# Score products of a chunked linear recurrence on TensorE: eight batches a head become four

## The chip, the cores and the metric

The kernel runs on one core of one Trainium2 chip. The metric is the device time of one execution, in microseconds (us); the time before is the median of three runs.

## The reference, cut to what matters

Two layers act on 256 context tokens and 512 latent tokens of width 1024. Layer 0 is a bidirectional gated linear recurrence with 16 heads (key size 128, value size 128), layer 1 a gated linear scan; each has an RMS norm, an adaLN modulation from a condition vector, and a gated residual. The change lies in layer 0. Per head, token t reads token s of its chunk with a decay that is a product of forget gates between s and t, per key channel:

```python
b = jnp.cumsum(gc, axis=2)
diff = b[:, :, :, None, :] - b[:, :, None, :, :]
decay = jnp.exp(jnp.where(lower_tri, diff, -jnp.inf))
scores = jnp.einsum('bhtk,bhsk,bhtsk->bhts', qc, kc, decay)
o = (jnp.einsum('bhts,bhsv->bhtv', scores, vc)
     + jnp.einsum('bhtk,bhkv->bhtv', qc * jnp.exp(b), S))
```

The adaLN step is `sc @ ada_w[i] + ada_b[i]`, split in shift, scale and gate.

## The kernel before

Tokens lie along the free dimension (768 of them, six chunks of 128), channels along the 128 partitions. Weights come from memory in tiles of 128 x 1024 (`raw`); ScalarE rounds each to `hi`, VectorE takes the rest `lo`, and each projection is three matmuls (`mm3`, lines L311 to L313: hi by hi, hi by the rest, rest by hi).

`hgrn(h, side)` computes a head. The scores of a chunk are built without an exponential of a difference: level l (0 to 6, B = 2^l) gives the products between neighbouring blocks of B tokens. For that, `KK` (keys of both directions) and `QQ` (queries of both directions) are multiplied in place, level by level, by the gates of the blocks, whose products are the tiles `T`. One level is:

- TensorE: the products `lv` (L460), 24 small column-tiled matmuls of 32 keys by 32 queries (12 of 64 by 64 in level 6), with the gathered keys `kt` as weights and a view of `QQ` as the moving side; they go to four column groups of the array (`tile_position`). `dg` (L440) are the products of the diagonal, made the same way ahead of level 0.
- VectorE: the update of `KK` (L464), the next `T` (L469), the update of `QQ` (L471; it has to wait until the products of this level have read `QQ`), and for levels 0 to 4 a masked copy of the products into `D` (L474).
- ScalarE: the gather of the next level's keys from `KK` into `kt` (L415), and for levels 5 and 6 the copy of the products into the score tile `A` (L479); after level 4 it copies `D` into `A` (L483).

While head h is in `hgrn`, TensorE's main work is the filler: projections of head h + 1 (`in`, `v`) and output projections of earlier heads (`o`). `interleave` hands out filler in proportion to the weights that `hgrn` yields; the yields of the levels are the places where filler goes between batches. In some heads a `side` generator advances one adaLN step (`ada_block`: four column-tiled matmuls at L230, later four transposes `adat` at L240) at each level:

```python
next(side, None)
```

The engines run their queues in order. A planning layer sets each engine's order from the program order and its own estimate of readiness. PSUM tiles of `dg`, `lv`, `ada`, `kT`, `U` and `o` come from one pool of four (`atile`), those of the filler from another of four (`dtile`).

## Time and profile before

| | |
|---|---|
| median of 3 runs | 1603.09 us (1602.52 to 1603.98) |
| profiled execution, its time | 1605.08 us |
| its span, first to last instruction | 1603.3 us |
| TensorE busy | 1549.6 us, 97% of the span |
| VectorE busy | 1203.0 us, 75% |
| ScalarE busy | 856.5 us, 53% |
| mean granted TensorE clock | 0.985 of full |

Busy time counts an instruction from its start to its modelled end, so the starts of neighbouring matmuls tell more about TensorE than their durations do. In the timeline, "x48" means that many records in a row from one line and tile; a matmul of 32-bit floats appears as two records (two passes), so 24 products are 48.

### The profile page before, as it was taken

How to read it: one execution, taken by the hardware profiler on the slowest of the kernel's cores; microseconds unless marked ns; L12 is line 12 of the kernel's file. 1: busy time of each engine (PE TensorE's matmuls, PEld its weight loads, DVE VectorE, ACT ScalarE, POOL GpSimd, SP SyncE). 2: the span in 40 equal slices, each digit the busy share in tenths (PEclk: the TensorE clock that was granted, in tenths of full speed). 3: DMA queues.
4: the chain of work that ended last, by engine and by line, in shares of the span. 5: the costliest groups of instructions: out<-in, count | busy, mean ns of one | idle time of the engine just before them, and what ended most of it. 6: DMA issues, size and time to landing. Idle time of an engine off the chain costs nothing.

```text
span 1603.3 us, 33990 instructions
## 1 busy us (share of the span) xinstructions
PE 1549.6 (97%) x14740; PEld 1430.2 (89%) x14740; DVE 1203.0 (75%) x1867; ACT 856.5 (53%) x1359; POOL 11.8 (1%) x16
## 2 busy tenths in 40 slices
PE   5999999999999999999999999998999999999995
PEld 3899999999999999999999999987888888888884
DVE  4767678768867867767876776686768887797898
ACT  4554444444443453444444445544578578667874
POOL 0000000000000000000000000001000000000001
PEclk9999999999999999999999999997999999999997
DMA  8231211110211211223132231301122222322211
GB/s 323 84 115 53 94 54 40 54 54 28 77 44 41 67 40 54 61 86 106 39 109 58 76 120 29 105 28 53 53 67 79 67 79 66 93 64 68 80 53 53
DMA packets 33861, 116.79 MB, mean 73 GB/s; under 512 B 3633, under 2 KB 6065, under 8 KB 33713
## 3 DMA queue, kind: packets, MB, share of 16 engines
q1 hardware_dynamic: 32192, 113.26, 22.4%
q8 instruction: 116, 1.90, 0.5%
q10 hardware_dynamic: 1520, 1.37, 0.3%
q14 instruction: 33, 0.26, 0.1%
HBM read 112.52 MB, written 2.10 MB: 71 GB/s over the span
## 4 chain that ended last, share of the span: by engine, by line
PE 85%; DVE 9%; ACT 3%; issue 1%; DMA 0%; POOL 0%; POOLq 0%; DVEq 0%; ACTq 0%
PE in L311 12%; PE in L312 11%; PE in L313 11%; PE v L381 8%; PE lv L460 4%; PE o L536 4%; PE r L313 3%; PE r L311 3%; PE r L312 3%; PE o L311 3%; PE o L312 3%; PE o L313 3%; PE U L504 2%; PE gt L311 2%; PE gt L312 2%; PE gt L313 2%
## 5 line engine op out<-in xcount | busy, mean ns | idle before, releaser
L311 PE MATMUL in<-h_hi,hi 128*128 128x384 f32 x1024 | 354.8, 348 | 3.4 <-ACT h_hi L304 2.7
L312 PE MATMUL in<-h_lo,hi 128*128 128x384 f32 x1024 | 345.9, 338 | 0.4 <-DVE h_lo L305 0.3
L313 PE MATMUL in<-h_hi,lo 128*128 128x384 f32 x1024 | 345.0, 337 | 0.0
L129 ACT ACTIVATE hi<-raw 128x1024 fp32r<-128x1024 f32 x160 | 168.4, 1057 | 167.3 <-PE in L312 59.5
L130 DVE TENSOR_TENSOR lo<-raw,hi 128x1024 fp32r<-128x1024 f32 x160 | 194.9, 1219 | 77.1 <-ACT hi L129 76.9
L311 PEld LDWEIGHTS in<-h_hi,hi 128*128 128x128 f32 x1024 | 192.7, 188 | 20.2 <-issue 8.6
L312 PEld LDWEIGHTS in<-h_lo,hi 128*128 128x128 f32 x1024 | 193.1, 189 | 2.9 <-issue 1.6
L313 PEld LDWEIGHTS in<-h_hi,lo 128*128 128x128 f32 x1024 | 192.7, 188 | 0.9 <-issue 0.4
L471 DVE TENSOR_TENSOR QQ<-QQ,T 128x768 f32<-128x768 f32 x112 | 117.6, 1050 | 73.3 <-PE lv L460 73.3
L415 ACT ACTIVATE kt<-KK 128x768 f32<-128x768 f32 x112 | 102.2, 913 | 54.3 <-DVE KK L464 46.7
L313 PE MATMUL r<-h_hi,lo 128*128 128x512 f32 (+1 forms) x344 | 123.8, 360 | 3.7 <-DVE lo L130 3.7
L464 DVE TENSOR_TENSOR KK<-KK,T 128x768 f32<-128x768 f32 x112 | 117.1, 1045 | 9.6 <-ACT kt L415 9.5
L312 PE MATMUL r<-h_lo,hi 128*128 128x512 f32 (+1 forms) x344 | 123.2, 358 | 0.0
L337 ACT ACTIVATE sg<-in 128x384 f32<-128x384 f32 x128 | 61.7, 484 | 115.0 <-PE in L313 114.8
L311 PE MATMUL r<-h_hi,hi 128*128 128x512 f32 (+1 forms) x344 | 123.0, 358 | 0.0
L381 PE MATMUL v<-hi,h_hi 128*128 128x256 f32 x384 | 112.3, 292 | 0.0
L381 PE MATMUL v<-lo,h_hi 128*128 128x256 f32 x384 | 107.4, 280 | 0.0
L381 PE MATMUL v<-hi,h_lo 128*128 128x256 f32 x384 | 107.4, 280 | 0.0
L405 DVE SCALAR_TENSOR_TENSOR x<-o,ada,x 128x256 f32<-128x256 f32 (+1 forms) x184 | 82.1, 487 | 12.9 <-PE o L313 12.5
L559 DVE RECIPROCAL sq<-sq 128x384 f32<-128x384 f32 x30 | 75.9, 2540 | 21.0 <-ACT sq L553 21.0
L311 PE MATMUL o<-rhi,hi 128*128 128x384 f32 (+2 forms) x240 | 87.0, 364 | 2.2 <-DVE lo L130 1.2
L460 PEld LDWEIGHTS lv<-QQ,kt 128*32 128x32 f32 (+1 forms) x4992 | 63.4, 113 | 28.6 <-issue 20.8
(202 smaller groups left out, 3257.8 us busy)
## 6 DMA issues: line engine op xcount, KB each, us to landing
raw<-in_hgw_dram SPq DMA_DIRECT2D x64, 512.0 KB, 3.7
raw<-in_ada_dram SPq DMA_DIRECT2D x48, 512.0 KB, 4.3
raw<-in_rgi_dram SPq DMA_DIRECT2D x32, 512.0 KB, 4.1
raw<-in_hgv_dram SPq DMA_DIRECT2D x16, 512.0 KB, 3.9
raw<-in_hgo_dram SPq DMA_DIRECT2D x16, 512.0 KB, 3.8
raw<-in_rgg_dram SPq DMA_DIRECT2D x16, 512.0 KB, 3.6
raw<-in_rgo_dram SPq DMA_DIRECT2D x16, 512.0 KB, 3.9
x<-in_x_dram SPq DMA_DIRECT2D x8, 384.0 KB, 5.9
```

The costliest lines, as they stand in the source:

```text
L129: self.nc.scalar.activation(hi, r, AF.Copy)
L130: self.nc.vector.tensor_tensor(lo, r, hi.bitcast(F32), ALU.subtract)
L311: PE.matmul(ps, lhsT=wh, rhs=xh, start=first and i == 0, stop=False, skip_group_check=skip)
L312: PE.matmul(ps, lhsT=wh, rhs=xl, start=False, stop=False, skip_group_check=skip)
L313: PE.matmul(ps, lhsT=wl, rhs=xh, start=False, stop=last and i == n - 1, skip_group_check=skip)
L381: PE.matmul(ps, lhsT=xh[:, kk, t], rhs=w[:, k], start=part == 0 and k == 0 and i == 0 and c % 2 == 0, stop=part == 1 and k == 3 and i == 2 ...
L405: V.scalar_tensor_tensor(xs, ps[:, a - c.start:b - c.start], gate[:, d, 1 - j:2 - j], xs, ALU.mult, ALU.add)
L415: A.activation(view(kt, 0, [[2 * B, n], [B, 2], [1, B]]), view(KK, 0, [[2 * B, n], [NT + B, 2], [1, B]]), AF.Copy)
L460: PE.matmul(ps[w * g:w * g + w, w * c:w * c + w], lhsT=kt[:, o:o + w], rhs=rhs, start=c == 0, stop=c == NC - 1, skip_group_check=True, til ...
L464: V.tensor_tensor(kv, kv, view(T, 1, [[2, n], [m - 1, 2], [0, B]]), ALU.mult)
L471: V.tensor_tensor(qv, qv, view(T, m + 1, [[2, n], [-m - 1, 2], [0, B]]), ALU.mult)
L559: V.reciprocal(rs, rs)
```

## The change

Levels are taken two by two. At an odd level (1, 3, 5) nothing goes to TensorE; its queries are copied out of `QQ` into a tile of their own, `qt`, before `QQ` is updated, and its keys stay in their `kt`. At the following even level (2, 4, 6) the products of both levels are issued back to back. The diagonal products are issued just ahead of level 0, with no yield between. The adaLN step is called at even levels only, so four times a head, behind the joint batch; what is left of it runs at the end of the head. The scores are read from PSUM (masked copies, copies into `A`) after the even level's updates. A pool of two buffers is added for `qt`, and the scratch for dynamically issued DMA is made smaller.

```diff
-    qqp, kkp, gsp, ktp = p0("qqp", 2), p0("kkp", 2), p0("gsp", 2), p0("ktp", 3)
+    qqp, kkp, gsp, ktp, qtp = p0("qqp", 2), p0("kkp", 2), p0("gsp", 2), p0("ktp", 3), p0("qtp", 2)
...
-        A.activation(D, ps[:, :32 * NC].rearrange("p (c t) -> p c t", c=NC), AF.Copy)
-        yield 1.5
-        T = s["T0"]
-        for l in range(NLEV):
+        def products(l, kt, qt):
             B = 1 << l
-            n = NT // (2 * B)
-            m = NT // B
             ps = atile(f"lv{h}_{l}")
             w = 64 if B == 64 else 32
             for c in range(NC):
                 for g in range(P // w):
                     o = P * c + w * g
-                    if B < 32:
+                    if qt is not None:
+                        rhs = qt[:, o:o + w]
+                    elif B < 32:
                         rhs = view(QQ, o, [[2 * B, 16 // B], [NT + B, 2], [1, B]])
...
+        def scores(l, ps):
...
+        T = s["T0"]
+        waiting = None
+        for l in range(NLEV):
+            B = 1 << l
+            n = NT // (2 * B)
+            m = NT // B
+            first = l % 2 == 1
+            if first:
+                qt = qtp.tile([P, NT], F32, name=f"qt{h}_{l}", tag="qt")
+                if B == 32:
+                    A.activation(view(qt, 0, [[2 * B, n], [1, B]]), view(QQ, NT + B, [[2 * B, n], [1, B]]), AF.Copy)
+                    A.activation(view(qt, B, [[2 * B, n], [1, B]]), view(QQ, 0, [[2 * B, n], [1, B]]), AF.Copy)
+                else:
+                    gather(QQ, qt, B)
+                waiting = (l, kt, qt)
+            else:
+                pss = [(waiting[0], products(*waiting))] if waiting else []
+                pss.append((l, products(l, kt, None)))
+                next(side, None)
+                if l == 0:
+                    A.activation(D, dg[:, :32 * NC].rearrange("p (c t) -> p c t", c=NC), AF.Copy)
+            kv = view(KK, 0, [[2 * B, n], [NT + B, 2], [1, B]])
+            V.tensor_tensor(kv, kv, view(T, 1, [[2, n], [m - 1, 2], [0, B]]), ALU.mult)
+            if l < NLEV - 1:
+                kt = ktp.tile([P, NT], F32, name=f"kt{h}_{l + 1}", tag="kt")
+                gather(KK, kt, 2 * B)
...
+            qv = view(QQ, 0, [[2 * B, n], [NT + B, 2], [1, B]])
+            V.tensor_tensor(qv, qv, view(T, m + 1, [[2, n], [-m - 1, 2], [0, B]]), ALU.mult)
+            if not first:
+                for x in pss:
+                    scores(*x)
             T = T2
-            yield 4.0 - 0.3 * l
+            yield 4.0 - 0.3 * l + (1.5 if l == 0 else 0)
...
-    nc = _bacc.Bacc("TRN2", target_bir_lowering=False, num_devices=1)
+    nc = _bacc.Bacc("TRN2", target_bir_lowering=False, num_devices=1, dynamic_dma_scratch_size=1024)
```

The function `kgather` is renamed `gather`, since it now copies queries too. Numbers behind names are buffer numbers.

TensorE's order in head 4, at levels 1 and 2 (`in` are projections of head 5), before:

```order
L313 MATMUL in_0_1_3915<-h_hi,lo_3755 128x384
L460 MATMUL lv_1_3943<-QQ_3471,kt_1_3894 32x32 x24
L311 MATMUL in_1_0_3983<-h_hi,hi_3850 128x384
...
L313 MATMUL in_1_0_3983<-h_hi,lo_3851 128x384
L460 MATMUL lv_2_4012<-QQ_3471,kt_2_3969 32x32 x24
L311 MATMUL in_1_1_4044<-h_hi,hi_3850 128x384
```

and in the changed kernel:

```order
L313 MATMUL in_1_0_3990<-h_hi,lo_3914 128x384
L460 MATMUL lv_1_4019<-qt_1_3974,kt_1_3905 32x32 x24
L460 MATMUL lv_2_4044<-QQ_3473,kt_2_3977 32x32 x24
L311 MATMUL in_1_1_4077<-h_hi,hi_3913 128x384
L312 MATMUL in_1_1_4077<-h_lo,hi_3913 128x384
```

The 24 projection matmuls that stood between the two levels now stand ahead of both. The same holds for the diagonal and level 0, for levels 3 and 4, and for levels 5 and 6 in heads 1 to 14; head 0 keeps its diagonal products apart, and the last head, whose filler is short, keeps its levels apart.

ScalarE's order in head 4 around levels 4 and 5 (`sg` are sigmoids of head 5's projections, `hi` weight splits), before:

```order
L415 ACTIVATE kt_6_4231<-KK_3213 128x768
L337 ACTIVATE sg_2_0_4136<-in_2_0_4111 128x384
L483 ACTIVATE A_3820<-D_3821 32x6x32 x4
L129 ACTIVATE hi_4255<-raw_4247 128x1024
L337 ACTIVATE sg_2_1_4201<-in_2_1_4176 128x384
```

and in the changed kernel:

```order
L337 ACTIVATE sg_2_0_4145<-in_2_0_4120 128x384
L416 ACTIVATE kt_6_4244<-KK_3213 128x768
L490 ACTIVATE qt_5_4240<-QQ_3473 128x12x32
L477 ACTIVATE A_3851<-D_3852 32x6x32 x4
L491 ACTIVATE qt_5_4240<-QQ_3473 128x12x32
L129 ACTIVATE hi_4264<-raw_4256 128x1024
L337 ACTIVATE sg_2_1_4236<-in_2_1_4211 128x384
```

The two half copies of level 5's queries are new, and the four copies of `D` stand between them.

VectorE's order in the changed kernel behind the joint batch of levels 3 and 4 in head 4 (L344 and L345 belong to the gates of head 5; L468 is the masked copy, L502 the `KK` update, L509 the `QQ` update):

```order
L344 TENSOR_SCALAR T_5_3988<-sg_2_0_4145,lbt 128x384
L468 COPY_PREDICATED D_3852<-masks,lv_3_4149 128x6x32
L345 TENSOR_SCALAR KK_3989<-T_5_3988 128x384
L509 TENSOR_TENSOR QQ_3473<-QQ_3473,T_4_4111 128x24x2x16
L468 COPY_PREDICATED D_3852<-masks,lv_4_4174 128x6x32
L502 TENSOR_TENSOR KK_3213<-KK_3213,T_4_4246 128x6x2x64
L509 TENSOR_TENSOR QQ_3473<-QQ_3473,T_4_4202 128x12x2x32
```

Before, the update of `QQ` for one level and that for the next had a batch of products between them; now both follow one batch.

## Rows read from the trace of the kernel before

**Rows 1.** Busy times of the page: engine, busy us, share, instructions.

```profile
PE 1549.6 (97%) x14740; PEld 1430.2 (89%) x14740; DVE 1203.0 (75%) x1867; ACT 856.5 (53%) x1359; POOL 11.8 (1%) x16
```

**Rows 2.** Windows: stretch, length, busy us per engine (instructions), granted clock, DMA share, GB/s.

```profile
core 0: us, PE busy (x) PEld busy (x) DVE busy (x) ACT busy (x) POOL busy (x), PEclk, DMA share, GB/s
...
76.00:1045.00 969.00, 967.91 (x11301) 920.97 (x11299) 713.05 (x1171) 454.40 (x790) 0.00 (x0) 1.00 0.22 67
```

**Rows 3.** Timeline of TensorE, head 4, level 2: start us, us, instruction.

```profile
355.30 0.34 PE L313 MATMUL in<-h_hi,lo 128*128 128x384 f32 x1
...
355.82 0.34 PE L313 MATMUL in<-h_hi,lo 128*128 128x384 f32 x1
356.09 0.63 PE L460 MATMUL lv<-QQ,kt 128*32 128x32 f32 x48
356.65 0.44 PE L311 MATMUL in<-h_hi,hi 128*128 128x384 f32 x1
356.93 0.33 PE L312 MATMUL in<-h_lo,hi 128*128 128x384 f32 x1
```

**Rows 4.** The same view, head 4, level 6 (64-wide tiles).

```profile
373.47 0.34 PE L313 MATMUL o<-rhi,lo 128*128 128x384 f32 x1
373.74 0.92 PE L460 MATMUL lv<-QQ,kt 128*64 128x64 f32 x24
...
374.87 0.34 PE L312 MATMUL o<-rlo,hi 128*128 128x384 f32 x1
```

**Rows 5.** The same view, head 9, level 1 with an adaLN step behind it.

```profile
672.49 0.34 PE L313 MATMUL in<-h_hi,lo 128*128 128x384 f32 x1
672.75 0.61 PE L460 MATMUL lv<-QQ,kt 128*32 128x32 f32 x47
673.17 0.40 PE L230 MATMUL ada<-raw,sc 128*32 128x256 f32 x2
...
674.03 0.34 PE L312 MATMUL in<-h_lo,hi 128*128 128x384 f32 x1
```

**Rows 6.** The same view, an adaLN step by itself in the first stage.

```profile
36.96 0.34 PE L313 MATMUL in<-h_hi,lo 128*128 128x384 f32 x1
37.23 0.64 PE L230 MATMUL ada<-raw,sc 128*32 128x256 f32 x8
...
38.08 0.34 PE L313 MATMUL in<-h_hi,lo 128*128 128x384 f32 x1
```

**Rows 7.** The same view, head 9, level 4 with the adaLN transposes behind it.

```profile
688.83 0.63 PE L460 MATMUL lv<-QQ,kt 128*32 128x32 f32 x48
689.39 1.05 PE L240 MATMUL adat<-cst,blk 128*128 128x2 f32 x8
```

**Rows 8.** Groups by line and form: count, busy us, mean ns of one, idle before.

```profile
L471 DVE TENSOR_TENSOR QQ<-QQ,T 128x768 f32<-128x768 f32 x112 | 117.6, 1050 | 73.3 <-PE lv L460 73.3
...
L415 ACT ACTIVATE kt<-KK 128x768 f32<-128x768 f32 x112 | 102.2, 913 | 54.3 <-DVE KK L464 46.7 <-PE lv L460 3.7 <-DVE spt L650 2.4
...
L337 ACT ACTIVATE sg<-in 128x384 f32<-128x384 f32 x128 | 61.7, 484 | 115.0 <-PE in L313 114.8
...
L344 DVE TENSOR_SCALAR T<-sg,lbt 128x384 f32<-128x384 f32 x64 | 30.4, 476 | 16.1 <-ACT sg L337 15.8
...
L474 DVE COPY_PREDICATED D<-masks,lv 128x192 f32<-128x192 uint8 x80 | 29.6, 370 | 0.0
...
L483 ACT ACTIVATE A<-D 32x192 f32<-32x192 f32 x64 | 23.1, 361 | 33.8 <-DVE D L474 33.2
...
L345 DVE TENSOR_SCALAR KK<-T 128x384 f32<-128x384 f32 x64 | 22.5, 353 | 0.2
...
L492 ACT ACTIVATE KK<-kT 128x384 f32<-128x384 f32 x32 | 16.0, 501 | 12.8 <-PE kT L490 12.8
...
L574 ACT ACTIVATE rhi<-sq 128x384 fp32r<-128x384 f32 x14 | 14.0, 1000 | 10.3 <-DVE sq L561 10.3
```

**Rows 9.** Timeline of TensorE, head 5, from level 5 to level 6.

```profile
435.08 0.63 PE L460 MATMUL lv<-QQ,kt 128*32 128x32 f32 x48
...
437.24 0.57 PE L460 MATMUL lv<-QQ,kt 128*64 128x64 f32 x12
```

## The prediction

> **What bounds the kernel now.** First the busy times of the page: TensorE is busy 97% of the span, VectorE 75%, ScalarE 53% [rows 1]. [...] So the question is whether some of its busy time is not work, and that is seen only in its timeline.

> Read the visit to the score products of one level [rows 3]. Ahead of it the projection's matmuls (128 x 384, full width) start every 0.173 us (three steps from 355.30 to 355.82). Then 0.27 us pass until the first product, 0.56 until the first projection matmul behind them, and 0.28 until the second. From 355.82 to 356.93 it is 1.11 us, of which two steps of 0.173 would have passed anyway: the visit costs 0.76 us.

> How much of that are the 48 product records (24 products, each in two passes)? In the heads with an adaLN step its four column-tiled matmuls stand right behind the products. There the first of them starts 0.42 us after the first product, when 47 of 48 records have started [rows 5], so one more set of 24 costs about 0.43. The rest, 0.76 - 0.43 = 0.33 us, is paid for going into the visit and coming out.

> The same answer comes from the adaLN matmuls. Alone between projections they cost 1.12 - 0.35 = 0.77 us [rows 6]. Behind products the two cost 1.54 - 0.35 = 1.19 together [rows 5], so 1.19 - 0.76 = 0.43 for the adaLN part: 0.34 saved by sharing.

> **The change, part by part.**

> *Fewer visits.* By the order on TensorE, before has the diagonal products and the seven levels in eight visits a head (seven in the last head, where the first two already touch). After: heads 1 to 14 have four. Head 0 has five, because its diagonal products still stand ten matmuls ahead of level 0. The last head gains nothing and has one visit more, because one product of level 5 stands two matmuls ahead of the rest. So 14 visits vanish between diagonal and level 0, 15 between levels 1 and 2, 15 between 3 and 4, and 15 between 5 and 6. The first three kinds join products of one shape, which is the case of rows 5: 44 less 1, at 0.33 = **14.2 us**.

> *Levels 5 and 6* differ: level 6 has tiles 64 wide. No row of before shows a step from 32-wide to 64-wide tiles. Level 6 alone costs 1.40 - 0.35 = 1.05 us [rows 4]. From below: the step costs all that a visit's two ends cost, and nothing is saved. From above: it costs nothing, and 0.33 is saved. Nearest is a step from these products to any other kind of matmul. To the projection it is 0.56 us from the first product to the next kind [rows 3], and to the full-width adaLN transposes 0.56 as well [rows 7]. With that, a joint visit is 0.27 + 0.56 + 1.13 (level 6's first product to the second projection matmul, [rows 4]) - 0.35 = 1.61, against 0.76 + 1.05 = 1.81 apart. I take 0.20 each, 15 times: **3.0 us** (0 to 5.0).

> [...]

> *adaLN steps* move from the visits of levels 0 to 3 to the four joint visits, in eight heads. Three of the four share a visit as before. The fourth now stands behind the 64-wide products: 0.27 + 0.85 (37.23 to 38.08, [rows 6]) + 0.85 (level 6's 1.13 less the 0.28 to the second projection matmul) - 0.35 = 1.62, less 1.05 for level 6 = 0.57, where it cost 0.43. That loses 0.14 eight times, **1.1 us** (0 to 2.7, if nothing is shared). The transposes (adat) now stand alone at the head's end; they are full width, and the products leave for them as they leave for projections [rows 3, 7], so nothing is lost.

> *Copies of the queries.* 32 copies of 128 x 768 and 32 half ones come new to ScalarE. The same gather of keys takes 0.91 us; a dense half copy 0.50, and one that strides to the grid order 1.00 [rows 8]. I take 0.91 and 0.50, as these too run over pieces in order: 45 us on an engine that has 515 idle [rows 2]. They cost TensorE nothing while the next visit still finds its operands ready. VectorE's work stays as it is; its update of QQ at an odd level now waits for a copy instead of for TensorE.

> *Is the next visit's operand in time?* The tightest gap is that from levels 3 and 4 to 5 and 6. Count from the first product of level 3. TensorE: two sets 0.43 + 0.56 = 0.99; 24 projection matmuls 0.28 + 23 x 0.173 = 4.26; then twelve of the value projection, 2.16 - 0.56 = 1.60 with the way in [rows 9], less 0.11 that rows 9 hold for coming out of a visit: next product at 6.7 us (7.4 with twelve of the output projection at 0.173). The chain, in the new order on VectorE and ScalarE [rows 8]: the sigmoid (0.48) of the half that ended just before, by 0.6; then on VectorE 0.48 (L344), 0.37 (masked copy of level 3), 0.35 (L345), 1.05 (QQ update of level 4), 0.37 (masked copy of level 4); on ScalarE four copies of D into A at 0.36, which stand between the two half copies, and the second half copy, 0.50; on VectorE the QQ update of level 5, 1.05. The query copy is ready at 5.2, 1.5 us early; QQ for level 6 at 6.2, where the products want it at 6.7 + 0.43: 0.9 us early. With a half copy of 1.00 it is 0.4 early. In the gap before it the chain is some 7.1 us (sigmoid and the same VectorE rows, a KK update as long as QQ's, the key gather and the query copy at 0.91 each, QQ) against 0.99 + 48 x 0.173 + 0.1 = 9.4; the first gap has 72 matmuls. So I cost this at **0**. Behind the waiting second half copy stand a weight split (hi) and a sigmoid on ScalarE; their users come a whole tile later.

> *Scratch:* no instruction, 0.

> **Sum.** 14.2 + 3.0 - 1.1 = 16.1 us. Against the profiled execution's 1605.08 (span 1603.3) that gives 1589.0; this execution lies 2.0 above the median of the three runs, so against the median 1603.09 it gives **1587.0 us**. The ends of the unknown prices: 14.2 + 5.0 - 0 = 19.2 and 14.2 + 0 - 2.7 = 11.5, or 1583.9 to 1591.6. Under 0.2% (3.2 us) a measurement of this kernel can't tell a difference from none.

> **Rivals.**

> *The chain comes late (slower).* Four joint visits want two levels of VectorE and ScalarE work done between them, with one wait in the place of two. If VectorE reaches the third visit with two operations as long as a QQ update (1.05 each) and a pair L344, L345 of the next head (0.83) still to do [rows 8], 2.9 us, the chain is 2.0 late. TensorE is in order, so 14 heads lose it each: 28 us, 1603.1 - 16.1 + 28 = 1615. It decides from 1.15 us late per head on (16.1 / 14). For it: the tight gap has 0.9 us of margin. Against it: VectorE is idle 26% of this stage [rows 2]. Chance 0.05. Lateness of some tenths, 2 to 8 us in all: 0.10, 1589 to 1595.

> *The change doesn't do what it says.* The 0.33 us belong to every set of products (a new PSUM tile, new keys) and not to the visit. Then nothing is saved: 1603. Against it: the adaLN matmuls also go to a tile of their own with weights of their own, and share [rows 5, 6]. Chance 0.04.

> *Any change of tile width costs a whole way out and in.* Then levels 5 and 6 save nothing and the fourth adaLN step loses 0.34: 11.5 us, 1591.6. For it: the ways in and out cost this much at the full-width border. Against it: the step in rows 7 costs no more than a way out. Chance 0.11.

> **Chances and range.** The forecast as it stands, 1583.9 to 1590, has 0.70: its own range. The rivals have 0.11, 0.10, 0.04 and 0.05. The range leaves out the last two and the ends of the others: 1582 to 1595. Faster by over 0.2%: 0.91; within 0.2%: 0.04; slower: 0.05.

> **What the profile after would show.** Four visits a head in TensorE's timeline; in each joint visit of one shape 0.43 to 0.45 us from the first record of one set to the first of the other; head to head (the period from one diagonal batch to the next) 1.2 us shorter; TensorE's busy share unchanged at 97%, since this overhead counts as busy; ScalarE busy some 45 us longer; no wait of the products (lv) on qt or QQ in heads 1 to 14. The step into level 6 shows the 0.13 us that the sum holds, or 0.33. Wrong would be: a gap before lv of levels 5 and 6 in each head, ended by ScalarE or VectorE; or projections that wait for hi and lo because ScalarE's copies come first.

## The result and the profile after

The changed kernel takes 1584.8 us (median of 4 runs, 1583.76 to 1586.59) where the kernel before took 1603.29 beside it (1602.52 to 1603.98): a ratio of 0.9889, 95% interval 0.9877 to 0.9902, so 18.5 us faster. The profiled execution took 1585.53 us, its span 1583.7. The forecast was 1587.0, 1582 to 1595.

Busy times of the page after, against [rows 1]: TensorE is as busy in share (97%) and 18.8 us shorter with the same 14740 matmuls, and ScalarE has 47.4 us and 64 instructions more.

```profile
PE 1530.8 (97%) x14740; PEld 1429.7 (90%) x14740; DVE 1208.6 (76%) x1867; ACT 903.9 (57%) x1423; POOL 11.8 (1%) x16
```

Where the time went is read from windows cut at the first diagonal product of heads 0, 2, 9 and 14 and at the first `rl` projection of layer 1 (that of the latent tokens; the stretch from head 14 to there is called the last heads and the seam). Columns as in [rows 2]. Before:

```profile
74.96:212.70 137.74, 136.78 (x1606) 129.50 (x1605) 96.18 (x168) 66.10 (x117) 0.00 (x0) 1.00 0.26 82
212.70:662.37 449.67, 449.67 (x5143) 433.28 (x5142) 342.40 (x556) 207.67 (x361) 0.00 (x0) 1.00 0.16 49
662.37:996.71 334.34, 334.34 (x3915) 315.47 (x3914) 240.84 (x396) 152.99 (x267) 0.00 (x0) 1.00 0.26 80
996.71:1125.69 128.98, 120.21 (x1377) 109.21 (x1377) 98.25 (x171) 63.50 (x113) 6.83 (x6) 0.92 0.19 58
1125.69:1603.28 477.59, 453.53 (x2330) 398.95 (x2328) 382.35 (x494) 326.65 (x450) 4.77 (x6) 0.98 0.22 69
```

After:

```profile
75.38:210.42 135.04, 135.04 (x1607) 130.02 (x1606) 96.59 (x165) 72.05 (x125) 0.00 (x0) 1.00 0.26 83
210.42:651.85 441.43, 441.43 (x5144) 432.88 (x5143) 345.42 (x559) 228.22 (x389) 0.00 (x0) 1.00 0.17 51
651.85:980.90 329.05, 329.05 (x3915) 316.52 (x3914) 243.03 (x393) 169.94 (x290) 0.00 (x0) 1.00 0.26 81
980.90:1106.22 125.32, 116.40 (x1378) 107.59 (x1377) 97.90 (x172) 67.34 (x119) 6.86 (x6) 0.95 0.19 60
1106.22:1583.75 477.53, 453.33 (x2330) 398.62 (x2328) 382.62 (x494) 326.68 (x450) 4.77 (x6) 0.98 0.22 69
```

Heads 0 and 1 gain 2.70 us, heads 2 to 8 gain 8.24, heads 9 to 13 gain 5.29; the start loses 0.42. The last two heads with the seam to layer 1 gain 3.66, and there the mean granted clock is 0.95 where it was 0.92. The rest of layer 1 is unchanged. Together that is 19.5 us, 1.0 more than between the medians: the profiled execution of before lies 1.8 us above its median, that of after 0.7.

TensorE's timeline in the changed kernel (columns as in [rows 3]): in head 4 the diagonal and level 0, then levels 1 and 2, then levels 5 and 6; last, in head 9, level 6 with the adaLN step behind it.

```profile
336.35 0.34 PE L313 MATMUL in<-h_hi,lo 128*128 128x384 f32 x1
336.62 0.60 PE L442 MATMUL dg<-q,kd 128*32 128x32 f32 x46
...
337.07 0.70 PE L460 MATMUL lv<-QQ,kt 128*32 128x32 f32 x46
337.70 0.44 PE L311 MATMUL in<-h_hi,hi 128*128 128x384 f32 x1
337.98 0.34 PE L312 MATMUL in<-h_lo,hi 128*128 128x384 f32 x1
...
350.13 0.34 PE L313 MATMUL in<-h_hi,lo 128*128 128x384 f32 x1
350.39 0.60 PE L460 MATMUL lv<-qt,kt 128*32 128x32 f32 x46
...
350.84 0.61 PE L460 MATMUL lv<-QQ,kt 128*32 128x32 f32 x46
351.38 0.44 PE L311 MATMUL in<-h_hi,hi 128*128 128x384 f32 x1
351.66 0.34 PE L312 MATMUL in<-h_lo,hi 128*128 128x384 f32 x1
...
367.12 0.34 PE L313 MATMUL o<-rhi,lo 128*128 128x384 f32 x1
367.39 0.63 PE L460 MATMUL lv<-qt,kt 128*32 128x32 f32 x48
367.95 0.92 PE L460 MATMUL lv<-QQ,kt 128*64 128x64 f32 x24
368.80 0.44 PE L311 MATMUL o<-rhi,hi 128*128 128x384 f32 x1
369.08 0.34 PE L312 MATMUL o<-rlo,hi 128*128 128x384 f32 x1
...
683.94 0.92 PE L460 MATMUL lv<-QQ,kt 128*64 128x64 f32 x24
684.79 0.64 PE L230 MATMUL ada<-raw,sc 128*32 128x256 f32 x8
```

They answer to [rows 3 to 6]. Read a visit as there, from the last projection matmul ahead to the second behind, less two steps of 0.173: levels 1 and 2 cost 1.53 - 0.35 = 1.18 us, diagonal and level 0 cost 1.28, levels 5 and 6 cost 1.61; levels 3 and 4, not shown, cost 1.24. From set to set it is some 0.45 (0.49 from level 3 to 4); from the first product of level 5 to the first of level 6 it is 0.56; from level 6 to adaLN 0.85.

One row of before is needed beside them, that of level 0 in head 4:

```profile
343.78 0.34 PE L313 MATMUL in<-h_hi,lo 128*128 128x384 f32 x1
344.05 0.72 PE L460 MATMUL lv<-QQ,kt 128*32 128x32 f32 x48
...
344.98 0.34 PE L312 MATMUL in<-h_lo,hi 128*128 128x384 f32 x1
```

Level 0 by itself cost 1.20 - 0.35 = 0.85 us, not the 0.76 of level 2.

The groups by line and form answer to [rows 8]. The `QQ` update waits 20.7 us in all, now for the query copy, where it waited 73.3 for TensorE. The query copies take 910 ns, and the first halves 526 (the second ones 525):

```profile
L509 DVE TENSOR_TENSOR QQ<-QQ,T 128x768 f32<-128x768 f32 x112 | 117.7, 1051 | 20.7 <-ACT qt L491 20.5
...
L416 ACT ACTIVATE qt<-QQ 128x768 f32<-128x768 f32 x32 | 29.1, 910 | 39.7 <-DVE QQ L509 38.1 <-DVE spt L679 1.5
...
L490 ACT ACTIVATE qt<-QQ 128x384 f32<-128x384 f32 x16 | 8.4, 526 | 17.3 <-DVE QQ L509 17.2
```

In heads 0 to 13 the view of waits names no wait of TensorE's matmuls. From 981 to 1106 us it names two kinds for the products, all in head 15: 0.3 us for a `QQ` update, and this (columns: what, on whom, us in all, times, longest):

```profile
PE lv L460 <- ACT qt L416: 2.5, 2, 1.6
```

### The profile page after: what moved, and what is told of

Its sections match the earlier page's. It is cut to its first block, busy times and chain, and to the rows that moved or that the text cites. A ratio compares the mean times of both kernels' runs of the same rounds, so it can differ in the third digit from the quotient of the medians.

```text
span 1583.7 us, 34061 instructions
## 1 busy us (share of the span) xinstructions
PE 1530.8 (97%) x14740; PEld 1429.7 (90%) x14740; DVE 1208.6 (76%) x1867; ACT 903.9 (57%) x1423; POOL 11.8 (1%) x16
## 4 chain that ended last, share of the span: by engine, by line
PE 87%; DVE 8%; ACT 2%; issue 1%; POOL 0%; DMA 0%; POOLq 0%; DVEq 0%; ACTq 0%
PE in L311 12%; PE in L312 11%; PE in L313 11%; PE v L381 9%; PE lv L460 4%; PE o L565 4%; PE r L313 3%; PE r L311 3%; PE r L312 3%; PE o L311 3%; PE o L312 3%; PE o L313 3%; PE U L533 2%; PE gt L311 2%; PE gt L312 2%; PE gt L313 2%
## 5 line engine op out<-in xcount | busy, mean ns | idle before, releaser
L311 PE MATMUL in<-h_hi,hi 128*128 128x384 f32 x1024 | 350.4, 343 | 3.4 <-ACT h_hi L304 2.8
L509 DVE TENSOR_TENSOR QQ<-QQ,T 128x768 f32<-128x768 f32 x112 | 117.7, 1051 | 20.7 <-ACT qt L491 20.5
L502 DVE TENSOR_TENSOR KK<-KK,T 128x768 f32<-128x768 f32 x112 | 117.3, 1047 | 9.7 <-ACT kt L416 8.2
L311 PE MATMUL gt<-xh,hi 128*128 128x384 f32 x256 | 85.6, 337 | 0.8 <-ACT xh L790 0.4
```

The lines of the kernel that those rows point to most:

```text
L311: PE.matmul(ps, lhsT=wh, rhs=xh, start=first and i == 0, stop=False, skip_group_check=skip)
L502: V.tensor_tensor(kv, kv, view(T, 1, [[2, n], [m - 1, 2], [0, B]]), ALU.mult)
L509: V.tensor_tensor(qv, qv, view(T, m + 1, [[2, n], [-m - 1, 2], [0, B]]), ALU.mult)
```

## The experiments

Each changes the kernel before or the changed kernel as its diff shows. The kernel before, run beside them, took 1603.04 us (e1 to e4), 1603.48 (e5 to e8) and 1603.39 (e9 to e11); the ratios are to that.

**e1: scratch alone.** The kernel before with the smaller scratch.

```diff
-    nc = _bacc.Bacc("TRN2", target_bir_lowering=False, num_devices=1)
+    nc = _bacc.Bacc("TRN2", target_bir_lowering=False, num_devices=1, dynamic_dma_scratch_size=1024)
```

> The kernel before with the small DMA scratch alone. Visits theory (the gain is the ways in and out of the product batches that are gone from TensorE): nothing changes, 1603 us within 0.1%. Rival, that the scratch or the other layout of SBUF gives part of the gain: some microseconds less than 1603, up to 18.

Measured: 1603.7 us, ratio 1.0001 (0.9992 to 1.001). The scratch changes nothing that can be measured.

**e2: all of the change but the joint visits.** The copies, their pool and the scratch stay; each level's products are issued at that level again.

```diff
+        A.activation(D, dg[:, :32 * NC].rearrange("p (c t) -> p c t", c=NC), AF.Copy)
+        yield 1.5
...
-                waiting = (l, kt, qt)
+                waiting = (l, products(l, kt, qt))
+                next(side, None)
```

> The changed kernel with each level's products, and the diagonal's, in a visit of their own again: the query copies, the freed VectorE updates, the later score copies and the scratch stay; the adaLN steps follow each level as before. Visits theory: as many visits as before (two more, where one product stands apart), so 1603 to 1605 us, with ScalarE busy some 45 us longer than before. Freed waits theory (VectorE's updates of QQ wait 73 us for products before and 21 after, and that is what TensorE gains): most of the gain stays, 1585 to 1592.

Measured: 1606.88 us, ratio 1.0017 (1.0008 to 1.0026). With the copies in place, nothing is won. Heads 0 to 13 are this window of its trace:

```profile
75.07:996.96 921.89, 920.91 (x10663) 878.16 (x10662) 682.70 (x1118) 463.26 (x800) 0.00 (x0) 1.00 0.21 65
```

Before, they took 921.75 us, so the copies cost nothing there; its 3 us more lie in the last two heads and the seam (131.36 for 128.98) and in layer 1 (478.00 for 477.59).

**e3: only diagonal and level 0 joined.** The kernel before with the scratch and this.

```diff
-        A.activation(D, ps[:, :32 * NC].rearrange("p (c t) -> p c t", c=NC), AF.Copy)
-        yield 1.5
+        dg = ps
...
+            if l == 0:
+                A.activation(D, dg[:, :32 * NC].rearrange("p (c t) -> p c t", c=NC), AF.Copy)
...
-            yield 4.0 - 0.3 * l
+            yield 4.0 - 0.3 * l + (1.5 if l == 0 else 0)
```

> The kernel before with the diagonal's products joined to level 0's (14 visits fewer) and the small scratch; no query copies. Visits theory: a joint visit of these two costs 1.28 us in the trace after, against 0.76 twice, so 0.25 to 0.29 saved 14 times: 3.5 to 4 us, 1599 to 1600. Freed waits theory: nothing is freed here, 1603.

Measured: 1598.16 us, ratio 0.9966 (0.9955 to 0.9977). Heads 2 to 8 are 2.52 us shorter than before (449.67), 0.36 for each visit that is gone:

```profile
212.61:659.76 447.15, 447.15 (x5143) 432.78 (x5142) 343.35 (x556) 207.23 (x361) 0.00 (x0) 1.00 0.16 50
```

No copy and no new wait is in this kernel, so the visit alone is what pays in the heads. By medians it gains 4.9 us, more than the 3.5 to 4 expected; in its trace 2.4 of them lie in the last heads and the seam (126.5 us for 128.98, at a mean clock of 0.96), which the visits don't explain.

**e4: level 5 in a visit of its own.** The changed kernel, with one of its four joints undone.

```diff
-                waiting = (l, kt, qt)
+                waiting = (l, products(l, kt, qt) if l == 5 else None, kt, qt)
...
-                pss = [(waiting[0], products(*waiting))] if waiting else []
+                pss = [(waiting[0], waiting[1] or products(waiting[0], *waiting[2:]))] if waiting else []
```

> The changed kernel with level 5's products in a visit of their own (all else joint). Visits theory with the prices of the prediction: 0.20 lost 15 times, 3 us more than the changed kernel, 1587.5 to 1588.5. If every change of tile width costs a whole way out and in: level 5 and 6 together had saved nothing, 1585.

Measured: 1592.98 us, ratio 0.9934 (0.9922 to 0.9947), 8 us more than the changed kernel, where 3 were expected for the visits theory and none for its rival. By windows, heads 2 to 8 take 442.67 us, 1.24 more than in the changed kernel, and heads 9 to 13 take 330.07, 1.02 more: 0.18 and 0.20 a head, as the step priced it. Of the rest, 4.4 us lie in head 0 and 0.9 in the last heads and the seam. TensorE's timeline in head 0 (a bracket is idle time, and what ended it):

```profile
105.08 0.25 PE L460 MATMUL lv<-qt,kt 128*32 128x32 f32 x2 [0.67 <-ACT qt L490]
106.99 0.61 PE L460 MATMUL lv<-qt,kt 128*32 128x32 f32 x46 [1.66 <-ACT qt L491]
...
107.82 0.52 PE L312 MATMUL in<-h_lo,hi 128*128 128x384 f32 x1
```

And a window of the same head (the granted clock is the number behind the last bracket):

```profile
107.80:111.20 3.40, 3.40 (x12) 3.40 (x12) 0.60 (x2) 1.13 (x4) 0.00 (x0) 0.50 0.00 0
```

Level 5's products, now one stretch of filler earlier, meet a query copy that isn't there: 2.33 us idle. Behind it half of the clock is granted for 3.4 us (all of it in the changed kernel), 1.7 us lost. With the 0.2 of the visit that is 4.2 of the 4.4.

**e5: three more copies on ScalarE ahead of level 5's half copies.** They make the chain late.

```diff
+N_EXTRA = 3
...
                 if B == 32:
+                    for _ in range(N_EXTRA):
+                        gather(QQ, qt, B)
```

> The changed kernel with three more copies of 128 x 768 on ScalarE ahead of the two half copies of level 5's queries (they write the same tile and are overwritten), 2.6 us in the chain that ends at levels 5 and 6. In the trace after, the QQ update of level 5 ends 1.3 us ahead of level 6's products in the heads with value projections behind level 5 and 2.0 us in the others. If a late chain is paid in full by TensorE: some 1.2 us in seven heads; in the others the order parts the batch again, 0.3 to 0.6 us; 10 to 14 us in all, 1595 to 1599. If lateness is taken up elsewhere: under 1588.

Measured: 1606.54 us, ratio 1.0023 (1.0013 to 1.0034): the whole gain is lost, 21.7 us more than the changed kernel, where 10 to 14 were expected. Head 4 at levels 5 and 6 in TensorE's timeline:

```profile
374.02 0.25 PE L461 MATMUL lv<-qt,kt 128*32 128x32 f32 x2 [0.64 <-ACT qt L493]
...
374.75 0.61 PE L461 MATMUL lv<-qt,kt 128*32 128x32 f32 x46
...
376.36 0.92 PE L461 MATMUL lv<-QQ,kt 128*64 128x64 f32 x24
```

The full copies take 0.87 us in the mean, three of them 2.6 a head. In the changed kernel the `QQ` update of level 5 ends 1.3 us (heads with `v` as filler) or 2.0 us (with `o`) ahead of level 6's first product, so 1.3 or 0.6 us should show, about 1.0 a head. Heads 2 to 8 take 451.25 us for 441.43: 1.4 a head. What is above 1.0 goes with the order, which has changed too: one product of level 5 alone, the other 23 two matmuls on, and level 6 five matmuls behind those, three visits in the place of one. So lateness and lost visits aren't separated here. Outside heads 2 to 8, heads 0, 1 and 9 to 13 lose 8.6 us in its trace, and the last heads with the seam 5.6, for which the expectation had nothing.

**e6: level 6 in 32-wide tiles.** The changed kernel, with 24 products of 32 keys by 64 queries in place of 12 of 64 by 64.

```diff
-            w = 64 if B == 64 else 32
+            w = 32
             for c in range(NC):
-                for g in range(P // w):
+                for g in range(4):
                     o = P * c + w * g
+                    if B == 64:
+                        r = QQ[:, 1, P * c + 64:P * c + P] if g < 2 else QQ[:, 0, P * c:P * c + 64]
+                        PE.matmul(ps[w * g:w * g + w, 64 * c:64 * c + 64], lhsT=kt[:, o:o + w], rhs=r, start=c == 0,
+                                  stop=c == NC - 1, skip_group_check=True, tile_position=(0, w * g))
+                        continue
```

> The changed kernel with level 6 in 24 products of 32 keys by 64 queries on 32-wide tiles, in the place of 12 of 64 by 64, so that no tile width changes within a visit. The step from level 5 to 6 should fall from 0.56 to 0.43-0.5 us, and the fourth adaLN step share again (1 us in all). What the longer moving side costs is open: if a product's time goes by its moving columns alone, 24 x 64 against 12 x 64 in half as many column groups is the same, and 2 to 3 us are gained, 1582; if it goes by the number of products, up to 0.17 x 15 is lost, 1584 to 1587.

Measured: 1582.16 us, ratio 0.9869 (0.9854 to 0.9884), the fastest of all. TensorE's timeline in head 4:

```profile
366.15 0.34 PE L313 MATMUL o<-rhi,lo 128*128 128x384 f32 x1
366.42 0.63 PE L465 MATMUL lv<-qt,kt 128*32 128x32 f32 x48
366.90 0.88 PE L454 MATMUL lv<-QQ,kt 128*32 128x64 f32 x48
367.71 0.45 PE L311 MATMUL o<-rhi,hi 128*128 128x384 f32 x1
367.99 0.34 PE L312 MATMUL o<-rlo,hi 128*128 128x384 f32 x1
```

Twice as many products on twice as many column groups, in both kernels six of 64 moving columns to a group, take no longer (0.81 us to the projection, 0.85 before), and the step into them is 0.48 us where it was 0.56. The visit costs 1.84 - 0.35 = 1.49 for 1.61. Heads 2 to 8 are 0.57 us shorter than in the changed kernel (440.86), heads 9 to 13, with an adaLN step behind, 1.17 (327.88).

**e7: three visits.** The changed kernel with levels 1 to 3 and levels 4 to 6 joined, and one more buffer of keys.

```diff
-            first = l % 2 == 1
+            first = l % 3 != 0
...
-                pss = [(waiting[0], products(*waiting))] if waiting else []
+                pss = [(x[0], products(*x)) for x in waiting]
+                waiting = []
```

> Three visits a head: diagonal and level 0; levels 1 to 3; levels 4 to 6, with one more keys buffer. Visits theory alone: 15 visits fewer than the changed kernel at 0.3, 4.5 us less, 1580. But the chains grow: three levels of VectorE and ScalarE work between visits, and three PSUM tiles of four at once. If that makes the third visit or the transposes behind it late by more than 0.3 us a head, the gain is eaten: 1585 or more.

Measured: 1599.74 us, ratio 0.9982 (0.9972 to 0.9991), 15 us behind the changed kernel. The wait that its trace names most often in the heads:

```profile
PE kT L520 <- ACT A L473: 4.7, 10, 0.6
```

The transposes at the head's end wait for the scores of three levels to be copied out of PSUM. Eight adaLN steps that shared a visit in the changed kernel now stand alone, at 0.34 us more each, 2.7 us. The waits named in the heads sum to 7.8 us; 1.6 of them, in head 9, are of the kind that e8 shows. That is some 10 of the 15; the rest isn't settled. By windows, heads 2 to 8 take 442.0 us, 0.6 more than in the changed kernel, and heads 9 to 13 take 337.7, 8.6 more, so most of the loss is in the heads with adaLN.

**e8: three visits, early.** Diagonal and levels 0 to 2, then 3 and 4, then 5, adaLN and 6, with two products in one PSUM tile.

```diff
-            first = l % 2 == 1
+            first = l in (0, 1, 3, 5)
...
+                if l == 2:
+                    diag()
+                    pss.append((0, products(*waiting[0], dgt, 32 * NC, False)))
...
+                ps = atile(f"lv{h}_{l}")
+                pss.append((l - 1, products(*waiting[0], ps, 0, True)))
```

> Three visits a head in another way: the diagonal with levels 0, 1 and 2 (level 0's queries are copied too, products two by two in one PSUM tile), then 3 and 4, then 5, an adaLN step, and 6. Visits theory: 14 or 15 visits fewer than the changed kernel at 0.3, and 1 us for the adaLN step: 5 us less, 1579 to 1581, if the longer score copies behind the first visit don't make the later work late; if they do by 0.3 us a head, 1584 to 1586.

Measured: 1593.35 us, ratio 0.9938 (0.9921 to 0.9955). Heads 2 to 4 are 0.5 us shorter each than in the changed kernel (62.49, 62.61 and 62.51 us). The forecast was 1579 to 1581, or 1584 to 1586 with late copies; neither came. Four idle stretches inside a batch, in heads 0, 5, 6 and 9, take the gain back; they sum to 10.1 us by the view of waits. That of head 5:

```profile
416.31 0.52 PE L461 MATMUL lv<-QQ,kt 128*32 128x32 f32 x36
419.18 0.28 PE L461 MATMUL lv<-QQ,kt 128*32 128x32 f32 x10 [2.34 <-issue]
```

"issue" means that no wait is recorded, and records of the same set, from the same two tiles, had run. All four stretches lie in the fourth set of the first batch, the longest in these kernels: head 5 asks there for four sets of 24 products, and from the first start of the first set (415.01 us) to that of the fourth (416.28) it is 1.27 us. The view of waits names one more stretch of this kind, 1.6 us at an adaLN step in e7. What TensorE lacked in the five is not shown by any run.

**e9, e10, e11: the last two heads.** They ask whether the 3.66 us of the last heads and the seam are won by their joint visits: e9 is the changed kernel with heads 14 and 15 apart, e10 the reverse (`h >= NH - 2`), e11 is e6 with heads 14 and 15 apart.

```diff
+        joint = h < NH - 2
+        if not joint:
+            A.activation(D, dg[:, :32 * NC].rearrange("p (c t) -> p c t", c=NC), AF.Copy)
+            yield 1.5
...
-            first = l % 2 == 1
+            first = joint and l % 2 == 1
```

> The changed kernel, but heads 14 and 15 issue their diagonal and every level as before, each in a visit of its own (heads 0 to 13 as changed). It asks where the 3.7 us come from that the changed kernel is shorter between the last-but-one head's start and the first projection of layer 1, and for which the sum of the prediction has no term. If the joint batches of the last two heads win them, 1584.8 + 3.7 = 1588.5 us and 129 us in that stretch. If they come with the granted clock of the seam and not from these batches, 1585 us and 125 us.

> The complement: only heads 14 and 15 take their levels two by two, heads 0 to 13 as before. If the joint batches of the last two heads win the 3.7 us: 1603.3 - 3.7 = 1599.6 us and about 125 us in the stretch. If not: 1603.3 us and 129 us. If both this kernel and the one with heads 14 and 15 apart have 125 us there, or both 129, the stretch goes by neither.

> The kernel with level 6 in 32-wide tiles (1582.2 us), with heads 14 and 15 apart. If the last two heads lose by their joint batches (head 14 is 2.6 us longer in the changed kernel, from one diagonal batch to the next), 1579.6 us; if they win the 3.7 us of the stretch, 1585.9 us.

Measured: e9 1585.21 us (ratio 0.9887, 0.9872 to 0.9902), e10 1601.96 (0.999, 0.9982 to 0.9999), e11 1584.39 (0.9885, 0.9872 to 0.9899). The windows from head 14's start to layer 1 follow, first that of e9:

```profile
980.31:1106.14 125.83, 117.69 (x1378) 107.37 (x1377) 97.24 (x171) 62.99 (x112) 6.83 (x6) 0.95 0.19 60
```

That of e10:

```profile
996.11:1121.48 125.37, 116.38 (x1377) 107.57 (x1377) 97.64 (x171) 67.60 (x120) 6.84 (x6) 0.95 0.19 60
```

That of e11:

```profile
978.74:1108.64 129.90, 120.03 (x1426) 108.60 (x1425) 98.37 (x174) 63.42 (x113) 6.83 (x6) 0.93 0.19 58
```

Apart (e9), the stretch takes 125.8 us, and joined (e10) 125.4, both at a mean clock of 0.95: the case in which it goes by neither. By medians the batches of the last two heads are worth between 0.4 us (e9 against the changed kernel) and 1.4 (e10, its interval from 0.2 to 2.9). e11 lies between its two forecasts. Its traced execution took 1588.32 us and the other three 1584.08 to 1584.55, so the 129.9 us at 0.93 tell of that execution and not of the batches.

What most of the 3.66 us go with is the granted clock. Twice in the stretch, each time among waits, it falls to half of full (0.50). The second time it stays there 10.2 us in both kernels; the first time 10.2 us before and 3.4 in the changed kernel:

```profile
1096.20:1106.40 10.20, 9.54 (x32) 7.89 (x32) 8.02 (x16) 3.77 (x9) 2.98 (x3) 0.50 0.36 122
...
1079.90:1083.30 3.40, 3.40 (x15) 3.33 (x16) 3.40 (x8) 1.95 (x5) 2.04 (x2) 0.50 0.44 148
```

Half of 6.8 us is 3.4 of the 3.66. The waits of TensorE around the first fall are the same in both (1.18, 0.86 and 0.66 us), so they don't tell why.

## Why the prediction was right

**The mechanism.** By the windows TensorE is busy for all of heads 2 to 13 in both kernels (784.01 us before, 770.48 after), with as many matmul records (9058 and 9059), so what was won there is busy time and not waiting. The gain is the way into and out of a visit. A quarter of it comes in e3 with 14 of the 58 visits and nothing else, and it stays away in e2 with everything but the visits. The rival by which the 0.33 us belong to each set of products is out. What in the change of kind costs the time is only in part separated: projections have operands rounded to fp32r and one record each, products two. On the way out this isn't it, since to the full-width transposes of [rows 7], with two records each as well, it takes the same 0.56 us as to a projection. On the way in, no run separates it from the column tiling.

**Joint visits of one shape, 0.33 each.** Levels 1 and 2 cost 1.18 us in the rows, where 0.76 + 0.43 = 1.19 was forecast. The diagonal with level 0 cost 1.28. The prediction put 0.76 on every level, and level 0 alone had cost 0.85, so the saving is 0.76 + 0.85 - 1.28 = 0.33 all the same; e3 gives 0.36 a head for this very joint. By heads the sum stands: 3 x 0.33 + 0.20 = 1.19 a head was forecast for heads without adaLN, 8.3 us over heads 2 to 8, and 8.24 was measured.

**Levels 5 and 6, 0.20 each.** The step was put at 0.56 us and is 0.56; the joint visit at 1.61, and it is 1.61; e4 gives 0.18 and 0.20 a head. In e6, where both sets are 32 wide with 64 moving columns in the second, the step takes 0.48 us. The joint visit at 1.61 us lies 0.20 under two visits apart, so what the step into 64-wide tiles costs is less than a whole way out and in, and that rival is out.

**adaLN, minus 0.14 each.** From level 6 to the adaLN step it is 0.85 us, as the sum held. Heads 9 to 13 were to gain 5 x 1.05 = 5.25 us and gained 5.29.

**Copies and the chain, 0.** e2 and the absence of any wait of the matmuls in heads 0 to 13 confirm both. The forecast margin of 0.9 us for level 6 was 1.3; 0.13 of the difference is the step from level 5 to 6, which this part of the prediction took at 0.43 and its own sum at 0.56. The late chain was a true danger: the prediction has the gain gone from 1.15 us a head on, and in e5 a loss of 1.4 a head over heads 2 to 8, part of it the parted batches, ends 0.2% slower than before.

**What the sum lacked.** 16.1 us were forecast and 18.5 measured, 19.5 in the profiled executions. In heads 2 to 13 the sum came out to 0.1 us; what it is short by has two sources. Heads 0 and 1 hold 0.72 (2 x 0.33 + 0.20 - 0.14, with the diagonal still apart) + 1.05 = 1.77 us of the sum, and 2.70 were won. In head 0 of before, level 1 waited for VectorE:

```profile
80.99 0.60 PE L460 MATMUL lv<-QQ,kt 128*32 128x32 f32 x47 [0.96 <-DVE spt L650]
```

Issued later, with level 2, it waits no more: 1.77 + 0.96 = 2.73. The sum made no allowance for this wait of before, though it asked of every new visit whether it would wait. The other part is the last heads with the seam, which gave 3.66 us in the profiled executions, where the sum's remaining 16.1 - 1.77 - 8.3 - 5.25 = 0.8 falls. 3.4 of the 3.66 go with the granted clock, for which the sum had no term. The clock differs between executions of one kernel too (the 24 of the kernel before beside e1 to e4 go from 1600.37 us at a mean of 0.989 to 1605.64 at 0.985), so how much of this part belongs to the change isn't known: by medians there is 1.0 less of it. Why the clock is granted for more or less of the seam stays open.

## What to carry to other kernels

An engine that is busy for all of a stage can still spend part of it on no work (here 0.33 us a visit): compare starts, not durations, around each change of matmul kind, and count the ways in and out. Join sets that need the same kind before shortening any of them, but keep the chain that feeds the joint batch ahead of it: in e5 a late chain, with the batches that it parted, took back the whole gain. Don't join without end either: both kernels with three visits in the place of four (1599.74 and 1593.35 us) were slower than that with four (1584.8), one with its head-end transposes waiting (4.7 us in all), one with TensorE idle inside the longest batch (10.1 us in all) and no wait recorded. In a change of order, look for waits of before that will go, as well as for those that may come.

## What the runs showed of the hardware

```profile
416.84:427.00 10.16, 7.82 (x54) 7.78 (x54) 7.95 (x14) 4.31 (x6) 0.00 (x0) 1.00 0.01 2
```

Five times (four in e8, each in the fourth set of its first batch, one in e7) TensorE stopped for 1.6 to 3.9 us with no wait recorded; why is not shown. And 24 matmuls of 32 keys by 64 queries on four column groups took no longer than 12 of 64 by 64 on two (0.81 and 0.85 us): the time did not go by the number of matmuls in all, which doubled, while each group had six of them in both.
